# Neighbourhood attention two blocks at a time, in an order of TensorE's queue written out by hand

## The chip, the cores and the metric

The kernel runs on one core of one Trainium2 chip, as one program. The metric is device time in microseconds (us), the median of several runs. TensorE (PE in the profile) multiplies, VectorE (DVE), ScalarE (ACT) and GpSimd (POOL) do the rest, SyncE (SP) issues the DMAs. Each engine runs its own queue in order and waits on semaphores.

## What is computed

Two layers of a hybrid network over 1024 latent tokens (a grid of 16 rows by 64 columns) and 256 context tokens, width 1024, all in f32. Each layer: norm and modulation; one input projection; an mLSTM group and a neighbourhood attention group side by side (8 heads of 64 each); an output projection; a squared-ReLU MLP. The part that matters here is the attention:

```python
def row_block(r):                       # one row of the grid, 64 queries
    rs = jnp.clip(r - kr_n // 2, 0, rows - kr_n)
    ...
    s_loc = jnp.einsum('bhqd,bhrkd->bhqrk', q_r, k_r) + bias      # 8 rows of keys
    s_loc = jnp.where(col_mask[:, None, :], s_loc, -jnp.inf)      # 16 columns of them
    s_ctx = jnp.einsum('bhqd,bhcd->bhqc', q_r, kch)               # 256 context keys
    p = jax.nn.softmax(jnp.concatenate([s_loc, s_ctx], -1), axis=-1)
    return einsum(p_loc, v_r) + einsum(p_ctx, vch)
...
if need_ctx:                            # layer 0 alone: the context attends to itself
    pc = jax.nn.softmax(einsum('bhqd,bhkd->bhqk', qch, kch), axis=-1)
```

## The kernel before

All the tokens' activations lie transposed in SBUF, 128 features to a tile, in three groups of columns: group 0 (context, 256 columns), groups 1 and 2 (latent tokens, 512 each). Every large product is made of three matmuls of rounded parts (lines 86 to 88: high by high, low by high, high by low), so each operand needs a cast on ACT (the high part) and a subtraction on DVE (the low part). One projection of a group (`qk_project`) is 24 matmuls, 256 or 512 wide, into one PSUM bank.

The attention of a layer (`na`) works through four pairs of heads. For each pair, `na_qk` yields up to six steps, one projection each: keys of groups 0, 1, 2, then queries of groups 0, 1, 2 (layer 1 has no queries of group 0, so five steps). After a projection, ACT and DVE cast it out of its bank. For the keys these are L729 and L730; for the queries L742 and L743 on ACT and two subtractions L745 on DVE, first for head 0, then the same again for head 1.

A pair has ten blocks of 128 queries in layer 0 (two of context, then eight tiles of the grid) and eight in layer 1. A block (`na_block`) has three stages, and the generator stops between them:

- scores: PE multiplies queries by context keys (L853, four matmuls) and by local keys (L863, four); DVE takes the negated maximum (L858, L864); ACT exponentiates (L868); DVE scales by the reciprocal sum (L869, L870). The bias comes by DMA into the tile `S` beforehand (L775).
- transposes: ten on PE (L878, L889, L897), four for a block of context; copies out of PSUM to `pc` (ACT), `pl` (DVE, L890) and `pl3` (ACT, L898).
- values: ten matmuls into one bank (L904), 64 columns of TensorE for each head; the trace has two records for each. DVE copies the result to `nyT` (L784).

The loop of `na` first runs all steps of pair 0's `na_qk`. Then, for each block, it moves the block two places back to its transposes, starts the scores of the new block, takes one step of the next pair's `na_qk` and runs the values of the block two places back. In the last pair that step is one of `ahead`, which loads output weights and the finished rows of `y` and makes the first four tiles of the output projection. Code order is only a priority: a scheduler (Tile) plans the order on every engine from its own costs, and may put any instruction earlier or later. So the projections of a pair lie a whole pair ahead of their use, and PE's order is the planner's.

There are eight PSUM banks: six of tag `q`, two of tag `mm` (after the start of a layer, projections use `mm`).

Of the kernel before, what the change touches and what calls it, by code (L numbers as in the profile page):

```python
# [25 lines left out]
KT = D // 128  # L26
# [20 lines left out]
class Kern:  # L47
# [700 lines left out]
    def na_blocks(self, l, pr, need_ctx):  # L748
# [17 lines left out]
        for hf in range(2):  # L766
            R, r0 = NROWS[hf], ROWS0[hf]
            yT = np_.tile([128, 512], F32, name="nyT", bufs=2)
            for cb in range(4):
# [6 lines left out]
                vt = np_.tile([128, 3, 128], F32, name="vt", bufs=3)  # L776
# [39 lines left out]
    def na(self, l, hi, lo, need_ctx, Wq, accs, last):  # L816

        run_all(self.fill)
        run_all(self.rows)
        self.wide = 1  # L820
        run_all(self.na_qk(l, 0, hi, lo, need_ctx, Wq, accs))
        self.wide = 0
        pending = []
        for pr in range(4):
            nxt = self.na_qk(l, pr + 1, hi, lo, need_ctx) if pr < 3 else last
            for n, blk in enumerate(self.na_blocks(l, pr, need_ctx)):
                if len(pending) == 2:
# [12 lines left out]
        for blk in pending:  # L840
            next(nxt, None)
            run_all(blk)
        run_all(nxt)

    def na_block(self, q, krhs, k, Rw, tb, vt, vc, put):
# [36 lines left out]
        if nl:  # L882
# [7 lines left out]
            nc.vector.tensor_copy(pl[:kw].rearrange("p a t -> p (a t)"), tp[:kw, :])  # L890
# [17 lines left out]
    def load_y(self, l, gi, hi, lo, ks=range(KT)):  # L908
# [949 lines left out]
```

## Time and profile before

| | |
|---|---|
| median of 3 runs | 2882.88 us (2878.18 to 2883.33) |
| span of the profiled execution, first to last instruction | 2883.5 us |
| PE busy | 2833.7 us, 98% |
| DVE busy | 2216.7 us, 77% |
| ACT busy | 1262.9 us, 44% |
| mean granted TensorE clock | 0.998 |

The page gives the profiled execution by its span; no time of its own stands beside it. The span lies 0.6 us above the median of the runs. A matmul's record shows its whole passage through the array (273 ns for a short one), and the records overlap, so the work done is read from the distance of starts and not from the busy time. Attention runs from about 457 to 690 us in layer 0 and from 1963 to 2190 us in layer 1.

### The profile page before, as it was taken

What the parts mean: (1) busy time and instruction counts of PE and PEld (TensorE: products, weight loads), DVE (VectorE), ACT (ScalarE), POOL (GpSimd) and SP (SyncE); (2) the same over time, 40 slices, a digit from 0 to 9 for tenths busy, and PEclk for the clock granted to TensorE, in tenths of its full rate; (3) what the DMA queues carried; (4) which work ended last, traced back from release to release, by engine and by line L of the source; (5) the groups of instructions that cost most, each with busy time, mean ns of one, the idle gap of its engine ahead of it and who ended that gap; (6) DMA issues with size and microseconds to landing.
All of it is one profiled execution on the core that took longest, in us unless ns stands there. A gap on an engine that the chain in (4) does not pass through costs nothing. (4 is left out here: it accounts for less than half of the span.)

```text
span 2883.5 us, 45724 instructions
## 1 busy us (share of the span) xinstructions
PE 2833.7 (98%) x16644; PEld 2402.4 (83%) x16644; DVE 2216.7 (77%) x5097; ACT 1262.9 (44%) x2426; POOL 67.3 (2%) x117
## 2 busy tenths in 40 slices
PE   8999999999999999999999999999999999999998
PEld 5888888888888888888889988888878788888888
DVE  7789987885798777599877778877786887759774
ACT  5333334564553333344544333335565533334453
POOL 0000000001000000000000000000010000000000
PEclk9999999999999999999999999999999999999999
DMA  7433332246447555798977222223256454478673
GB/s 248 164 123 105 113 115 78 91 125 217 150 157 235 188 197 198 273 334 288 313 260 252 67 88 73 74 62 105 88 169 199 132 190 144 154 252 312 212 252 102
DMA packets 278946, 497.42 MB, mean 173 GB/s; under 512 B 23328, under 2 KB 119584, under 8 KB 278720
## 3 DMA queue, kind: packets, MB, share of 16 engines
q1 hardware_dynamic: 278720, 494.49, 51.7%
q8 instruction: 131, 2.15, 0.3%
q14 instruction: 95, 0.78, 0.1%
HBM read 398.82 MB, written 95.59 MB: 171 GB/s over the span
## 5 line engine op out<-in xcount | busy, mean ns | idle before, releaser
L86 PE MATMUL q<-ah,whi 128*128 128x512 f32 (+1 forms) x1480 | 551.8, 373 | 2.6 <-ACT ah L955 1.9
L88 PE MATMUL q<-ah,wlo 128*128 128x512 f32 (+1 forms) x1480 | 550.2, 372 | 1.3 <-DVE wlo L956 1.3
L87 PE MATMUL q<-al,whi 128*128 128x512 f32 (+1 forms) x1480 | 550.7, 372 | 0.0
L86 PE MATMUL mm<-ah,whi 128*128 128x512 f32 (+1 forms) x1112 | 382.8, 344 | 1.5 <-ACT ah L914 1.5
L87 PE MATMUL mm<-al,whi 128*128 128x512 f32 (+1 forms) x1112 | 382.4, 344 | 0.4 <-DVE al L915 0.4
L88 PE MATMUL mm<-ah,wlo 128*128 128x512 f32 (+1 forms) x1112 | 382.1, 344 | 0.5 <-DVE wlo L81 0.5
L86 PEld LDWEIGHTS q<-ah,whi 128*128 128x128 f32 x1480 | 278.8, 188 | 52.3 <-ACT ah L955 2.7
L88 PEld LDWEIGHTS q<-ah,wlo 128*128 128x128 f32 x1480 | 278.8, 188 | 51.3 <-DVE wlo L956 2.1
L87 PEld LDWEIGHTS q<-al,whi 128*128 128x128 f32 x1480 | 278.9, 188 | 48.9 <-issue 1.4
L86 PE MATMUL mm<-whi,ah 128*128 128x512 f32 (+2 forms) x864 | 313.3, 364 | 0.9 <-DVE st L312 0.4
L87 PE MATMUL mm<-wlo,ah 128*128 128x512 f32 (+2 forms) x864 | 309.5, 359 | 0.2 <-DVE wlo L81 0.2
L88 PE MATMUL mm<-whi,al 128*128 128x512 f32 (+2 forms) x864 | 308.2, 357 | 0.0
L86 PEld LDWEIGHTS mm<-ah,whi 128*128 128x128 f32 x1112 | 210.5, 189 | 27.9 <-ACT ah L914 1.9
L88 PEld LDWEIGHTS mm<-ah,wlo 128*128 128x128 f32 x1112 | 210.6, 189 | 25.6 <-DVE wlo L81 1.0
L87 PEld LDWEIGHTS mm<-al,whi 128*128 128x128 f32 x1112 | 210.5, 189 | 25.0 <-DVE al L915 0.5
L955 ACT CAST ah<-raw 128x512 fp32r<-128x512 f32 (+1 forms) x264 | 142.9, 566 | 120.7 <-PE q L88 58.3
L86 PEld LDWEIGHTS mm<-whi,ah 128*128 128x128 f32 x864 | 163.6, 190 | 28.0 <-issue 3.1
L88 PEld LDWEIGHTS mm<-whi,al 128*128 128x128 f32 x864 | 163.8, 190 | 23.0 <-issue 0.7
L87 PEld LDWEIGHTS mm<-wlo,ah 128*128 128x128 f32 x864 | 163.9, 190 | 22.3 <-DVE wlo L81 0.4
L956 DVE TENSOR_TENSOR al<-raw,ah 128x512 fp32r<-128x512 f32 (+1 forms) x264 | 157.6, 621 | 23.5 <-ACT ah L955 23.0
L956 DVE TENSOR_TENSOR wlo<-raw,whi 128x1024 fp32r<-128x1024 f32 x84 | 102.4, 1222 | 74.4 <-ACT whi L955 71.9
L86 PE MATMUL q<-th,whi 128*128 128x512 f32 x384 | 150.5, 392 | 2.2 <-DVE s L1120 2.0
(287 smaller groups left out, 5249.4 us busy)
## 6 DMA issues: line engine op xcount, KB each, us to landing
raw<-w SPq DMA_DIRECT2D x168, 512.0 KB
raw<-hid SPq DMA_DIRECT2D x104, 512.0 KB
wada<-w_adaT SPq DMA_DIRECT2D x96, 512.0 KB
wraw<-w SPq DMA_DIRECT2D x80, 512.0 KB
hid<-hb SPq DMA_DIRECT2D x128, 256.0 KB
hid<-ht SPq DMA_DIRECT2D x96, 256.0 KB
gb<-gscr SPq DMA_DIRECT2D x36, 512.0 KB
wada<-w_ada SPq DMA_DIRECT2D x32, 512.0 KB
```

Source lines behind the costliest of these rows:

```text
L86: mm(out, lh, rh, start=start, stop=False, skip_group_check=True)
L87: mm(out, lh, rl, start=False, stop=False, skip_group_check=True)
L88: mm(out, ll, rh, start=False, stop=stop, skip_group_check=True)
L955: ins = self.nc.scalar.copy(hi, src)
L956: self.nc.vector.tensor_sub(lo, src, fview(hi))
```

## The change

1. The code of the blocks moves to `na_pairs`, which takes two blocks as a unit. For each new block, one block of the unit before it is transposed and the new one's scores are made; when both are through, the values of both blocks of the unit before run back to back.
2. Everything in `na_pairs` stands under `manual_schedule(engines={PE})`: PE's queue has exactly the order of the code there. The other engines are still planned.
3. Before the blocks only four steps of pair 0's projections run (layer 0: the keys and the queries of group 0; layer 1: the keys and the queries of group 1). The remaining queries of a pair are projected inside that pair, behind its blocks 0 and 2 (layer 1: behind block 0). The first four steps of the next pair follow behind blocks 4, 5, 7, 9 (layer 1: 2, 4, 5, 7).
4. `ahead` fetches the output weights a step before they are cast and loads `y` into two buffers of its own. Each of its output tiles is one unbroken run on PE.
5. The copy to `pl` moves from DVE to ACT; `vt` has five buffers, not three.

```diff
-                vt = np_.tile([128, 3, 128], F32, name="vt", bufs=3)
+                vt = np_.tile([128, 3, 128], F32, name="vt", bufs=5)
...
     def ahead(self, l, gi, xsrc, yh, yl, W, xt):
-        for i, _ in enumerate(self.w_out(l, 0, W)):
-            self.load_y(l, gi, yh, yl, range(2 * i, min(2 * i + 2, KT - 1)))
+        raw = []
+
+        def fetch():
+            raw.append(self.wp.tile([128, 1024], F32, name="wraw", bufs=WRAW))
+            self.nc.sync.dma_start(raw[-1][:], self.d["w_out"][l, len(raw) - 1])
+
+        for _ in range(WRAW):
+            fetch()
+        yield
+        for i in range(WB):
+            W.append(self.split_raw(raw[i], 1024))
+            if len(raw) < WB:
+                fetch()
+            self.load_y(l, gi, yh, yl, range(2 * i, min(2 * i + 2, KT - 1)), self.np_)
             yield
...
-            if f % 2:
-                yield
-        self.load_y(l, gi, yh, yl, range(KT - 1, KT))
+        self.load_y(l, gi, yh, yl, range(KT - 1, KT), self.np_)
+        yield
...
+        own = [self.na_qk(l, pr, hi, lo, need_ctx, *((Wq, accs) if pr == 0 else ())) for pr in range(4)]
         self.wide = 1
-        run_all(self.na_qk(l, 0, hi, lo, need_ctx, Wq, accs))
+        for _ in range(4):
+            next(own[0])
         self.wide = 0
-        pending = []
+        with self.tc.manual_schedule(engines={mybir.EngineType.PE}):
+            self.na_pairs(l, need_ctx, own, last)
+
+    def na_pairs(self, l, need_ctx, own, last):
+        behind, pair = [], []
+        mine, others = ((0, 2), (4, 5, 7, 9)) if need_ctx else ((0,), (2, 4, 5, 7))
         for pr in range(4):
-            nxt = self.na_qk(l, pr + 1, hi, lo, need_ctx) if pr < 3 else last
             for n, blk in enumerate(self.na_blocks(l, pr, need_ctx)):
-                if len(pending) == 2:
-                    next(pending[0])
+                if behind:
+                    next(behind[n % 2])
                 next(blk)
-                pending.append(blk)
-                if pr < 3 or not need_ctx or n > 1:
-                    next(nxt, None)
-                if len(pending) > 2:
-                    run_all(pending.pop(0))
-            if pr < 3 or not need_ctx:
-                run_all(nxt)
-        for blk in pending:
+                pair.append(blk)
+                if n in mine:
+                    next(own[pr])
+                elif pr < 3 and n in others:
+                    next(own[pr + 1])
+                if pr == 3 and n:
+                    next(last, None)
+                if len(pair) == 2:
+                    for b in behind:
+                        run_all(b)
+                    behind, pair = pair, []
+            run_all(own[pr])
+        for blk in behind:
             next(blk)
...
-            nc.vector.tensor_copy(pl[:kw].rearrange("p a t -> p (a t)"), tp[:kw, :])
+            nc.scalar.copy(pl[:kw].rearrange("p a t -> p (a t)"), tp[:kw, :])
...
-            y = self.wp.tile([128, 1024], F32, name="wraw", bufs=WRAW)
+            y = pool.tile([128, 512], F32, name="yraw", bufs=2) if pool else self.wp.tile(...)
```

On PE, the order outside the two attention stages is the same before and after. The three places below show the order within. In the names, `ah`, `al` are the activations' high and low parts, `whi`, `wlo` the weights', `nqc` and `nq` the cast queries of group 0 and of groups 1 and 2, `nk` the cast keys, `consts` the identity of a transpose. In the rows of the changed kernel L876 and L886 are the scores (L853 and L863 before), L901, L912 and L920 the transposes (L878, L889, L897), L927 the values (L904).

First place: PE at the start of layer 0's attention, before. The last matmuls of the query projection of group 0 are followed by both other query projections.

```order
L86 MATMUL q<-ah_108,whi 128x256
L87 MATMUL q<-al_132,whi 128x256
L88 MATMUL q<-ah_108,wlo 128x256
L86 MATMUL q<-ah_88,whi 128x512
...
L88 MATMUL mm<-ah_110,wlo 128x512
L853 MATMUL q<-nk_5110,nqc 128x256 x2
L853 MATMUL q<-nk_5111,nqc 128x256 x2
L86 MATMUL mm<-ah_87,whi 128x256
```

The same place after: the scores of block 0 (on `nqc`) stand right behind the projection that makes `nqc`, and those of block 2 (the first on `nq`) two short stages behind the projection that makes that `nq`.

```order
L88 MATMUL q<-ah_108,wlo 128x256
L876 MATMUL q<-nk_5110,nqc 128x256 x2
L876 MATMUL q<-nk_5111,nqc 128x256 x2
L86 MATMUL mm<-ah_88,whi 128x512
...
L88 MATMUL mm<-ah_109,wlo 128x512
L876 MATMUL q<-nk_5110,nqc 128x256 x2
L876 MATMUL q<-nk_5111,nqc 128x256 x2
L901 MATMUL q<-consts,S 128x128 x4
L876 MATMUL q<-nk_5110,nq 128x256 x2
L876 MATMUL q<-nk_5111,nq 128x256 x2
```

What moved: two runs of 24 matmuls, 512 wide, from ahead of the first scores to behind them. Layer 1 starts in the same way, with `nq` of group 1.

Second place: PE between pairs 0 and 1 of layer 1, after. The projection of pair 1's queries of group 1 is the run of 512-wide matmuls at the top; `nk_21024` and `nk_21025` are pair 1's keys, so the last rows are the scores of its block 0.

```order
L88 MATMUL mm<-ah_15377,wlo 128x512
L927 MATMUL q<-pc,vc 64x128 x4
...
L927 MATMUL q<-pl_21397,vt 64x128 x2
L901 MATMUL q<-consts,S 128x128 x4
L912 MATMUL q<-consts,S 128x128 x4
L920 MATMUL q<-consts,S 128x128 x2
L876 MATMUL q<-nk_21024,nq 128x256 x2
```

Before, that projection stood behind an earlier block of pair 0, with the values, transposes and scores of several blocks between it and its use. Now the values of two blocks and the transposes of one lie between.

Third place: PE in the middle of pair 0 of layer 0, before.

```order
L904 MATMUL q<-pc,vc 64x128 x4
L904 MATMUL q<-pl,vt 64x128 x4
L904 MATMUL q<-pl_5632,vt 64x128 x2
L878 MATMUL q<-consts,S 128x128 x4
L889 MATMUL q<-consts,S 128x128 x4
L897 MATMUL q<-consts,S 96x128 x2
```

The same place after: the values of two blocks without a break, then the transposes.

```order
L927 MATMUL q<-pc,vc 64x128 x4
L927 MATMUL q<-pl,vt 64x128 x4
L927 MATMUL q<-pl_5589,vt 64x128 x2
L927 MATMUL q<-pc,vc 64x128 x4
L927 MATMUL q<-pl,vt 64x128 x4
L927 MATMUL q<-pl_5641,vt 64x128 x2
L901 MATMUL q<-consts,S 128x128 x4
L912 MATMUL q<-consts,S 96x128 x4
```

What moved: the values of every second block, up to those of its partner. Counted over both layers, PE's order enters a run of values 75 times before (42 in layer 0, 33 in layer 1) and 37 times after (20 and 17).

More of the change, by code (lines that the diff above doesn't have):

```diff
@@ L819, in na @@
         run_all(self.rows)
+        own = [self.na_qk(l, pr, hi, lo, need_ctx, *((Wq, accs) if pr == 0 else ())) for pr in range(4)]
         self.wide = 1
-        run_all(self.na_qk(l, 0, hi, lo, need_ctx, Wq, accs))
+        for _ in range(4):
+            next(own[0])
         self.wide = 0
-        pending = []
+        with self.tc.manual_schedule(engines={mybir.EngineType.PE}):
[3 more added lines that the diff above has]
+        mine, others = ((0, 2), (4, 5, 7, 9)) if need_ctx else ((0,), (2, 4, 5, 7))
         for pr in range(4):
-            nxt = self.na_qk(l, pr + 1, hi, lo, need_ctx) if pr < 3 else last
             for n, blk in enumerate(self.na_blocks(l, pr, need_ctx)):
-                if len(pending) == 2:
-                    next(pending[0])
+                if behind:
+                    next(behind[n % 2])
                 next(blk)
-                pending.append(blk)
-                if pr < 3 or not need_ctx or n > 1:
-                    next(nxt, None)
-                if len(pending) > 2:
-                    run_all(pending.pop(0))
-            if pr < 3 or not need_ctx:
-                run_all(nxt)
-        for blk in pending:
+                pair.append(blk)
[11 more added lines that the diff above has]
+        for blk in behind:
             next(blk)
-        for blk in pending:
-            next(nxt, None)
+        for blk in behind:
+            next(last, None)
             run_all(blk)
-        run_all(nxt)
+        run_all(last)
     def na_block(self, q, krhs, k, Rw, tb, vt, vc, put):
@@ L905, in na_block, with load_y @@
         put(yp)
-    def load_y(self, l, gi, hi, lo, ks=range(KT)):
+    def load_y(self, l, gi, hi, lo, ks=range(KT), pool=None):
         nc = self.nc
@@ L911, in load_y @@
         for k in ks:
[L912 removed]
+            y = pool.tile([128, 512], F32, name="yraw", bufs=2) if pool else self.wp.tile([128, 1024], F32, name="wraw", bufs=WRAW)
             nc.sync.dma_start(y[:, :n], self.yscr[l][k * 128:(k + 1) * 128, g0:g0 + n])
```

## The prediction

> **What bounds the kernel now.** I read the page's first part, then busy time by stretch over the two attention stages, then PE, DVE and ACT in order of time where the changed order differs. The page's busy line shows one engine nearly always at work:
>
> ```profile
> PE 2833.7 (98%) x16644; PEld 2402.4 (83%) x16644; DVE 2216.7 (77%) x5097; ACT 1262.9 (44%) x2426; POOL 67.3 (2%) x117
> ```
>
> So only PE time counts: matmuls, switches between kinds of matmul, waits. The rows by stretch of layer 0's and layer 1's attention (columns: stretch, length, busy PE, PEld, DVE, ACT, POOL, clock, DMA):
>
> ```profile
> 457.00:690.00 233.00, 227.05 (x1878) 196.39 (x1877) 181.20 (x591) 137.17 (x319) 14.22 (x14) 1.00 0.36 107
> 1963.00:2190.00 227.00, 222.20 (x1715) 188.72 (x1714) 173.93 (x520) 128.62 (x271) 9.21 (x7) 1.00 0.40 124
> ```
>
> PE idles 233.00 - 227.05 = 5.95 and 227.00 - 222.20 = 4.80 us there, 10.75 together. Idle time understates a loss, since a record lasts longer than its turn. One wait in PE's timeline of layer 0, and the same products without one:
>
> ```profile
> 619.88 0.43 PE L863 MATMUL q<-nk,nq 128*128 128x288 f32 x2
> 620.89 0.53 PE L863 MATMUL q<-nk,nq 128*128 128x288 f32 x2 [0.58 <-ACT pc L879]
> ...
> 631.96 0.71 PE L853 MATMUL q<-nk,nq 128*128 128x256 f32 x4
> 632.51 0.69 PE L863 MATMUL q<-nk,nq 128*128 128x288 f32 x4
> 633.04 0.28 PE L86 MATMUL mm<-ah,whi 128*128 128x256 f32 x1
> ```
>
> Two products held PE from 619.88 to 620.89, 1.01 us; four take 632.51 to 633.04, 0.53, so two 0.27. The loss is 0.74 us for 0.58 shown, a factor 1.28. (Scores over the context take 631.96 to 632.51, 0.55 for four.) All waits are then 10.75 x 1.28 = 13.7 us. They lie where no projection fills PE: late in a pair and in the last pair.
>
> **Fewer visits to the value products.** PE's timeline around a lone block's values, and around two blocks' values in a row, which the planner made once, at the end of layer 1:
>
> ```profile
> 616.46 0.39 PE L87 MATMUL mm<-al,whi 128*128 128x512 f32 x1
> 616.69 0.39 PE L88 MATMUL mm<-ah,wlo 128*128 128x512 f32 x1
> 617.01 0.66 PE L904 MATMUL q<-pc,vc 128*64 128x128 f32 x8
> 617.50 0.83 PE L904 MATMUL q<-pl,vt 128*64 128x128 f32 x12
> 618.25 0.66 PE L878 MATMUL q<-consts,S 128*128 128x128 f32 x4
> 618.75 0.60 PE L889 MATMUL q<-consts,S 128*128 128x128 f32 x4
> ...
> 2176.35 0.60 PE L878 MATMUL q<-consts,S 128*128 128x128 f32 x4
> 2176.79 0.60 PE L889 MATMUL q<-consts,S 128*128 128x128 f32 x4
> ...
> 2178.63 0.66 PE L904 MATMUL q<-pc,vc 128*64 128x128 f32 x8
> 2179.11 0.83 PE L904 MATMUL q<-pl,vt 128*64 128x128 f32 x12
> 2179.77 0.61 PE L904 MATMUL q<-pc,vc 128*64 128x128 f32 x8
> ```
>
> Entering costs 0.09 us (616.69 to 617.01 is 0.32, the matmul before took 0.23). Leaving costs 0.09 (twelve records take 0.75 before a transpose, 0.66 before more values) and the four transposes behind take 0.50 instead of 0.44. That is 0.24 us a visit. The order has 75 visits before and 37 after: 38 x 0.24 = **-9.1 us**, all on PE. Bounds: 0.18 without the transposes (-6.8) and 0.30 with a slow first pair (-11.4, an estimate).
>
> **Waits that go.** The changed order spreads the projections: a 24-matmul run stands in nearly every unit of two blocks, and the output tiles of the last pair are fed by loads issued earlier. I take all 13.7 us as gone, **-13.7**, and set new waits against it. The bounds are -13.7 and, if half return, -6.9.
>
> **Waits that come: queries cast too late.** Here the change puts a projection just ahead of its user. The price is the time from a projection's last matmul to its last subtraction. ACT's, DVE's and PE's rows at layer 0's start, then ACT's, DVE's and PE's at layer 1's:
>
> ```profile
> 449.58 0.37 ACT L742 CAST nqc<-q 64x256 fp32r<-64x256 f32 x1 [1.66 <-DVE nqc L745]
> 451.40 0.58 ACT L742 CAST nq<-q 64x512 fp32r<-64x512 f32 x1 [1.07 <-PE q L88]
> 454.03 0.58 ACT L742 CAST nq<-q 64x512 fp32r<-64x512 f32 x1 [1.45 <-DVE nq L745]
> ...
> 447.95 0.69 DVE L730 SCALAR_TENSOR_TENSOR nk<-q,nk 64x512 fp32r<-64x512 f32 x1 [0.31 <-ACT nk L729]
> 448.68 0.87 DVE L745 TENSOR_TENSOR nqc<-q,nqc 64x256 fp32r<-64x256 f32 x2
> 450.36 0.89 DVE L745 TENSOR_TENSOR nqc<-q,nqc 64x256 fp32r<-64x256 f32 x2 [0.81 <-ACT nqc L743]
> 452.61 1.38 DVE L745 TENSOR_TENSOR nq<-q,nq 64x512 fp32r<-64x512 f32 x2 [1.37 <-ACT nq L743]
> 455.25 1.40 DVE L745 TENSOR_TENSOR nq<-q,nq 64x512 fp32r<-64x512 f32 x2 [1.26 <-ACT nq L743]
> ...
> 445.73 0.40 PE L86 MATMUL q<-ah,whi 128*128 128x512 f32 x1
> 451.20 0.39 PE L86 MATMUL mm<-ah,whi 128*128 128x512 f32 x1
> ```
>
> ```profile
> 1958.32 0.58 ACT L742 CAST nq<-q 64x512 fp32r<-64x512 f32 x1 [1.33 <-PE q L88]
> 1962.19 1.42 DVE L745 TENSOR_TENSOR nq<-q,nq 64x512 fp32r<-64x512 f32 x2 [1.26 <-ACT nq L743]
> 1958.12 0.39 PE L86 MATMUL q<-ah,whi 128*128 128x512 f32 x1
> ```
>
> ACT's casts for head 1 wait until DVE has subtracted for head 0, so the chain is serial: 451.40 to 456.65 and 1958.32 to 1963.61, 5.3 us, plus 0.2 us behind the last matmul. PE filled it with the next projection (445.73 to 451.20 is one, 5.47 us).
>
> - *Layer 0, block 0.* ACT's and DVE's order is unchanged up to here, so the trace gives the time itself: the projection ends at 445.73, head 0's `nqc` is ready at 449.55, head 1's at 451.25. With 0.27 for its products the scores end at 451.5 instead of 446.3 (445.73 + 0.55): **+5.2 us**, with nothing to fill it.
> - *Layer 0, block 2.* The next projection then ends near 457.0. Only block 1's scores (0.55) and four transposes (0.44) lie between. The chain, with block 1's maximum on DVE ahead of it, ends near 462.7 (an estimate: 457.0 + 0.2 + 5.3 and 0.2 of delay); the scores end near 463.5, and 459.1 was due: **+4.4**.
> - *Layer 1, block 0.* Ready at 1963.61 after a projection that ends at 1958.12; the scores end near 1964.4 where 1959.2 was due: **+5.2**.
> - *Layer 1, block 0 of pairs 1 to 3.* Cover: values of two blocks (1.24 + 1.14), ten transposes (0.50 and six at 0.11, 1.16), head 0's context scores (0.27), 3.8 us; chain 5.5: **3 x 1.7 = +5.1**.
> - *Layer 0, block 2 of pairs 1 to 3.* Cover: ten transposes, context scores, values of two blocks, four transposes, with head 0's scores of block 2 (0.27) 4.8 us; chain 5.5 and 0.1 of delay: **3 x 0.8 = +2.4**.
>
> If ACT and DVE ran the two heads side by side, the chain would be 0.2 + 4 x 0.58 and one subtraction (0.7) with some delay, 3.4 us: the low bound of all five. The high bound is another 0.5 us each for DVE's other work.
>
> **Free edits.** The copy to `pl` takes DVE 0.69 us and ACT takes 0.58 us for the same shape:
>
> ```profile
> L890 DVE COPY pl<-q 128x512 f32<-128x512 f32 x16 | 11.0, 689 | 3.2 <-PE q L889 3.1
> L879 ACT COPY pc<-q 128x512 f32<-128x512 f32 x40 | 23.1, 578 | 11.7 <-PE q L878 11.1
> ```
>
> ACT has the room: it is busy 137 of 233 us. In a unit with no projection it has little: three units (one in layer 0's last pair, two in layer 1's) may wait about 1 us each, as the pair of rows at 619.88 does: **+3**, between 0 and 6. The weight and `y` loads move on SP's queue past the bias loads; their users come several stages later, so 0. `vt`'s buffers: 0.
>
> **The granted clock.** Busy time by stretch around two short PE droughts elsewhere in this trace, with the wait in the second:
>
> ```profile
> 1624.80:1628.20 3.40, 1.48 (x9) 1.04 (x10) 3.32 (x9) 1.19 (x4) 0.10 (x1) 1.00 0.87 271
> 1628.20:1631.60 3.40, 3.40 (x18) 3.40 (x18) 2.87 (x3) 2.10 (x3) 0.00 (x0) 0.52 0.09 37
> 2276.80:2280.20 3.40, 2.45 (x8) 1.02 (x6) 3.40 (x7) 3.40 (x7) 0.00 (x0) 1.00 0.53 154
> 2283.60:2287.00 3.40, 1.37 (x7) 0.83 (x6) 3.40 (x7) 0.00 (x0) 0.00 (x0) 1.00 0.01 2
> 2287.00:2290.40 3.40, 3.40 (x9) 2.63 (x10) 3.40 (x7) 1.79 (x3) 0.00 (x0) 0.52 0.00 0
> 2286.84 0.59 PE L86 MATMUL q<-th,whi 128*128 128x512 f32 x1 [2.03 <-DVE s L1120]
> ```
>
> After 3.4 us in which PE was busy 1.4 to 1.5, the clock was 0.52 for the next 3.4; after 2.45 busy it stayed at 1.00. Half speed for 3.4 us loses 1.6 us. The three long waits (5.2, 4.4, 5.2) each make such a stretch: **3 x 1.6 = +4.8**, between 0 and 8.
>
> The Trainium skill, page "TensorE: Matmul & The Clock Gate", section "HAM oscillation — how this bites in real kernels", gives the rule as: no idle gap of PE over about 3.4 us. The trace differs, since a longest gap of 2.03 us was enough. By the page only layer 0's block 0, with one unbroken gap of 3.7 us, would pay, and the sum would be 3.2 us lower.
>
> **The sum.** -9.1 - 13.7 + 5.2 + 4.4 + 5.2 + 5.1 + 2.4 + 3.0 + 4.8 = +7.3 us on the span of 2883.5, 2890.8; the span is 0.6 above the runs' median, so 2890. A measurement of this kernel can tell about 0.2%, 5.8 us, from no change.
>
> **Rivals.**
> - *Faster.* The casts of the two heads run side by side in the new plan. The chain is 3.4 us, 2.1 less: the five terms become 3.1, 2.3, 3.1, 0 and 0, the clock drops once, 1.6: -22.8 + 8.5 + 3.0 + 1.6 = -9.7, 2873. It decides below a chain of about 3.8 us. Against it: both chains quoted were serial. Chance 0.12.
> - *No change: the clock holds.* The waits come, but each holds a few matmuls in its middle (head 0's scores), and only the unbroken gap halves the clock: 2890 - 3.2, 2887. This is what the page's rule makes of it. For it: head 0 is ready halfway. Against: the 2.03 us gap. With milder waits at the pairs' borders, the cases within 0.2% have 0.33.
> - *Slower still.* The fixed order makes many small waits, since PE can no longer put a projection's matmuls into a hole; half of the 13.7 us stay: 2897. For it: before, the planner split output tiles around such holes. Chance 0.15; the forecast itself has 0.40.
>
> The range 2878 to 2902 runs from the sum without the clock, the 3.0 and the 2.4 and with -11.4 for the visits (-5.2, 2878) to half of the old waits, twice the new 3.0 and one more halving of the clock (+18.8, 2902).
>
> **What would show it.** Right: PE idle for over 4 us between layer 0's first query projection and the second, and again ahead of block 2's scores; over 4 us ahead of layer 1's first scores; releasers DVE `nq` and `nqc`; the clock below 1 behind them; 37 visits; little idle late in the pairs. Wrong: short chains (DVE `nq` soon after the projection), a clock of 1.00 throughout, or old waits on `pc`, `pl` and `S` in full.

## The result, and the profile after

The changed kernel takes 2924.22 us (median of 4 runs, 2921.61 to 2927.05) against 2882.51 us before: a ratio of 1.0146, 95% interval 1.0132 to 1.0161. It is 41.7 us slower, and 2890 us was forecast, with 2902 as the upper end. The profiled execution took 2923.64 us, its span 2921.9.

The page's busy line after, and the rows by stretch that answer to those of before (columns as there):

```profile
PE 2842.3 (97%) x16644; PEld 2415.5 (83%) x16644; DVE 2180.9 (75%) x5033; ACT 1292.3 (44%) x2490; POOL 67.4 (2%) x117
```

```profile
457.00:690.00 233.00, 214.50 (x1715) 187.39 (x1715) 157.30 (x526) 144.22 (x327) 14.54 (x14) 0.99 0.34 102
1963.00:2190.00 227.00, 212.73 (x1593) 183.93 (x1593) 153.04 (x499) 135.82 (x293) 9.03 (x7) 0.97 0.39 117
```

PE idles 18.5 us in the first stretch, where it idled 5.95, and 14.3 in the second, where it idled 4.80; its clock is below 1 in both. (Both stages now end behind these stretches: PE's last value products start at 708.5 and 2209.6 us.) PE does the same matmuls, so three that stand in the same order on both sides give the loss by stage. They are the last products ahead of each layer's query projections and one behind layer 1's attention, first in PE's timeline of before, then of after:

```profile
442.64 0.38 PE L678 MATMUL q<-consts,hs 128*128 128x128 f32 x2
1952.43 0.39 PE L678 MATMUL q<-consts,hs 128*128 128x128 f32 x2
2220.15 1.02 PE L268 MATMUL mm<-ssq,ones 128*128 128x512 f32 x2
```

```profile
442.79 0.38 PE L678 MATMUL q<-consts,hs 128*128 128x128 f32 x2
1973.32 0.39 PE L678 MATMUL q<-consts,hs 128*128 128x128 f32 x2
2259.59 1.02 PE L268 MATMUL mm<-ssq,ones 128*128 128x512 f32 x2
```

Ahead of layer 0's attention the two are 0.15 us apart, behind its layer 20.9, behind layer 1's attention 39.4. The loss lies in the two attention stages and just behind them.

**The starts: as forecast, and a longer half clock.** PE's timeline after, at layer 0's start:

```profile
445.75 0.28 PE L88 MATMUL q<-ah,wlo 128*128 128x256 f32 x1
449.38 1.00 PE L876 MATMUL q<-nk,nqc 128*128 128x256 f32 x2 [3.35 <-DVE nqc L745]
450.98 1.10 PE L876 MATMUL q<-nk,nqc 128*128 128x256 f32 x2 [0.60 <-DVE nqc L745]
451.88 0.63 PE L86 MATMUL mm<-ah,whi 128*128 128x512 f32 x1
456.57 0.43 PE L88 MATMUL mm<-ah,wlo 128*128 128x512 f32 x1
...
461.81 0.38 PE L876 MATMUL q<-nk,nq 128*128 128x256 f32 x1 [1.15 <-DVE nq L745]
464.55 0.58 PE L876 MATMUL q<-nk,nq 128*128 128x256 f32 x1 [1.58 <-DVE nq L745]
466.59 0.63 PE L86 MATMUL mm<-ah,whi 128*128 128x512 f32 x1
```

Block 0's scores end at 451.88; without a wait they would end at 446.4 (445.75, one matmul, 0.55), so 5.5 us late. The matmuls behind them follow each other at 0.43 us and not 0.23 (452.31 is the second) up to 456.6: 2.3 us lost to the clock. Block 2's scores are late by 5.1 us, and 1.7 us of half clock follow. Layer 1 starts in the same way, 5.9 us late, with this row as its longest wait and 1.6 us of half clock behind it; the second row is ACT's at layer 0's start, where head 1's casts still wait for head 0's subtractions:

```profile
1981.14 0.39 PE L876 MATMUL q<-nk,nq 128*128 128x256 f32 x1 [1.98 <-DVE nq L745]
...
449.71 0.37 ACT L742 CAST nqc<-q 64x256 fp32r<-64x256 f32 x1 [1.66 <-DVE nqc L745]
```

Rows by stretch show the granted clock at these three places, and at a fourth that comes below. It is 0.50 for 6.8 us each time:

```profile
449.80:456.60 6.80, 6.18 (x15) 4.61 (x16) 2.60 (x10) 1.74 (x6) 0.00 (x0) 0.50 0.34 96
463.45:470.25 6.80, 5.47 (x15) 4.43 (x16) 4.30 (x14) 1.85 (x5) 0.00 (x0) 0.50 0.00 0
1982.40:1989.20 6.80, 5.17 (x14) 4.19 (x15) 4.30 (x14) 2.13 (x6) 0.00 (x0) 0.50 0.47 139
2149.65:2156.45 6.80, 6.04 (x16) 4.85 (x17) 4.08 (x14) 3.17 (x8) 1.28 (x1) 0.50 0.65 197
```

The first part of each falls on the late scores themselves and is counted with them; the 2.3, 1.7 and 1.6 us are only what the projection behind them loses.

**The bare stretches: what I had not seen.** Between the projection behind block 2 and the one behind block 4, PE has only transposes, scores and values in layer 0. PE's timeline there in pair 1, then ACT's:

```profile
540.02 0.66 PE L927 MATMUL q<-pc,vc 128*64 128x128 f32 x8 [0.43 <-ACT pc L902]
541.99 0.64 PE L912 MATMUL q<-consts,S 128*96 128x128 f32 x4 [0.73 <-ACT pc L902]
545.38 0.59 PE L886 MATMUL q<-nk,nq 128*128 128x352 f32 x2 [1.72 <-ACT pl L913]
...
542.56 0.58 ACT L743 CAST nq<-mm 64x512 fp32r<-64x512 f32 x1
543.04 0.80 ACT L891 ACTIVATE S<-S,smax 128x608 f32<-128x608 f32 x1
544.75 0.58 ACT L913 COPY pl<-q 96x512 f32<-96x512 f32 x1
```

All three waits end with copies out of PSUM. The copy at 544.75 could start when its transposes were through at 542.5, but on ACT it stands behind the casts of the queries just projected and two exponentials. ACT had begun these casts late, behind the cast of a weight (537.23, 1.05 us). By the distance of starts PE loses 3.8 us here, and 3.9, 3.8 and 4.4 in the other three pairs. The stretch as a whole, the 54 us behind it, and within these a stretch that has no projection either:

```profile
537.20:545.90 8.70, 5.82 (x48) 4.57 (x47) 6.94 (x18) 6.88 (x13) 0.00 (x0) 1.00 0.44 133
546.00:600.00 54.00, 53.57 (x439) 47.79 (x438) 35.64 (x125) 31.46 (x74) 0.00 (x0) 1.00 0.29 87
568.50:575.50 7.00, 7.00 (x78) 6.64 (x78) 5.34 (x16) 4.95 (x10) 0.00 (x0) 1.00 0.31 99
```

In the first DVE and ACT are each busy for some 80% of the time, feeding each other in turn, and PE for 67%; in the second PE idles for 0.43 us in 54. The third row shows that the missing projection is not the whole matter: behind block 7's projection, of keys, PE works through 78 matmuls and never waits, while ACT is busy for 4.95 us in 7.00. Behind block 2's it has 48, since the values of the two context blocks are short, and ACT and DVE have the casts of the queries as well. Every unit of two blocks has a projection in pairs 0 to 2 of layer 0; the stretch that waits runs across the border of two units.

**The borders of layer 1's pairs.** PE's waits at the first border and in the unit behind it, then the two longest of those at the third, and ACT's row ahead of the casts there:

```profile
2037.87 0.38 PE L876 MATMUL q<-nk,nq 128*128 128x256 f32 x1 [0.81 <-DVE nq L745]
2038.69 0.36 PE L876 MATMUL q<-nk,nq 128*128 128x256 f32 x1 [0.44 <-DVE nq L745]
2047.58 0.59 PE L886 MATMUL q<-nk,nq 128*128 128x352 f32 x2 [0.68 <-ACT pc L902]
...
2147.52 0.38 PE L876 MATMUL q<-nk,nq 128*128 128x256 f32 x1 [0.59 <-DVE nq L745]
2150.17 0.58 PE L876 MATMUL q<-nk,nq 128*128 128x256 f32 x1 [1.49 <-DVE nq L745]
...
2145.06 0.62 ACT L937 CAST ah<-yraw 128x512 fp32r<-128x512 f32 x1 [3.29 <-DMA yraw<-yscr]
```

At the first two borders the scores are 1.8 us late (1.7 was forecast) and the unit behind loses another 1.3. At the third, ACT's queue holds a cast of `y` from `ahead` that waits until 2145.06 for its load, so the casts of the queries start at 2145.59, 2.3 us behind the product that follows their projection (0.1 us at the first border): the scores are 4.5 us late, 2.0 us of half clock follow, and the unit behind again loses 1.3.

**Behind layer 1's attention.** PE's wait, the casts on ACT that it and the loads wait for, and SP's weight loads:

```profile
2240.94 0.50 PE L86 MATMUL mm<-ah,whi 128*128 128x512 f32 x1 [3.64 <-ACT whi L80]
...
2208.44 1.05 ACT L80 CAST whi<-wraw 128x1024 fp32r<-128x1024 f32 x1 [5.86 <-PE mm L87]
2239.84 1.04 ACT L80 CAST whi<-wraw 128x1024 fp32r<-128x1024 f32 x1 [2.98 <-DMA wraw<-w_out]
...
2193.72 10.48 SPq L73 DMA_DIRECT2D wraw<-w_out  x2
2234.46 0.33 SPq L73 DMA_DIRECT2D wraw<-w_out  x1
```

The second half of the output weights is cast when the first output tiles give their buffers back (the row at 2208.44 was released by a matmul). Two of these tiles now stand behind the last values, so the two loads at 2193.72 hold SP for 10.48 us, all later loads come late, and PE waits 3.64 us for a weight that was issued at 2234.46. With the half clock behind it this costs 5.3 us.

### The profile page after: what moved, and what is told of

It reads as the page before. It is cut to its first block, busy times and chain, and to the rows that moved or that the text cites. A ratio compares the mean times of both kernels' runs of the same rounds, so it can differ in the third digit from the quotient of the medians.

```text
span 2921.9 us, 45716 instructions
## 1 busy us (share of the span) xinstructions
PE 2842.3 (97%) x16644; PEld 2415.5 (83%) x16644; DVE 2180.9 (75%) x5033; ACT 1292.3 (44%) x2490; POOL 67.4 (2%) x117
## 5 line engine op out<-in xcount | busy, mean ns | idle before, releaser
L86 PE MATMUL q<-ah,whi 128*128 128x512 f32 (+1 forms) x1464 | 545.6, 373 | 1.5 <-ACT ah L978 1.4
L88 PE MATMUL q<-ah,wlo 128*128 128x512 f32 (+1 forms) x1464 | 543.9, 372 | 1.0 <-DVE wlo L979 0.9
L87 PE MATMUL q<-al,whi 128*128 128x512 f32 (+1 forms) x1464 | 544.5, 372 | 0.0
L86 PE MATMUL mm<-ah,whi 128*128 128x512 f32 (+1 forms) x1128 | 392.2, 348 | 3.6 <-ACT whi L80 3.6
L88 PE MATMUL mm<-ah,wlo 128*128 128x512 f32 (+1 forms) x1128 | 391.2, 347 | 0.5 <-DVE wlo L81 0.5
L87 PE MATMUL mm<-al,whi 128*128 128x512 f32 (+1 forms) x1128 | 391.1, 347 | 0.0
L81 DVE TENSOR_TENSOR wlo<-wraw,whi 128x1024 fp32r<-128x1024 f32 (+2 forms) x90 | 107.7, 1199 | 76.3 <-ACT whi L80 62.0
```

The lines of the kernel that those rows point to most:

```text
L81: nc.vector.tensor_sub(lo[:, :n], raw[:, :n], fview(hi[:, :n]))
L86: mm(out, lh, rh, start=start, stop=False, skip_group_check=True)
L87: mm(out, lh, rl, start=False, stop=False, skip_group_check=True)
L88: mm(out, ll, rh, start=False, stop=stop, skip_group_check=True)
```

## The experiments

Each kernel is the changed one with the edit shown, unless it says otherwise. Times are medians; before took 2881.9 to 2882.6 us beside them.

**1. A projection inside the bare stretch.**

```diff
-        mine, others = ((0, 2), (4, 5, 7, 9)) if need_ctx else ...
+        mine, others = ((0, 2), (3, 5, 7, 9)) if need_ctx else ...
```

> One number changed: in layer 0 the next pair's first projection (keys of group 0, 24 matmuls 256 wide, 2.86 us of PE) stands behind block 3 and not behind block 4. Theory A (the loss is where PE has nothing but scores, transposes and values between two projections while ACT and DVE still work through a cast chain; in layer 0 that is from block 2's projection to block 4's, 3.8 to 4.4 us in each of four pairs): a projection inside this stretch covers 2 to 2.9 us of it in pairs 0 to 2 (pair 3 has none), so 6 to 9 us less than the changed kernel, 2915 to 2918 us. Theory B (ACT is the late engine, since it also copies pl): the same ACT work has to be done in the same place, the waits move on by two blocks, 2922 to 2926 us.

2916.82 us, ratio 1.0127 (1.0110 to 1.0143): 7.4 us less than the changed kernel. PE's timeline in the same stretch of pair 1 shows the waits that are left:

```profile
545.07 0.44 PE L901 MATMUL q<-consts,S 128*128 128x128 f32 x2 [0.61 <-DVE S L893]
546.24 0.42 PE L920 MATMUL q<-consts,S 128*96 128x128 f32 x2 [0.29 <-ACT pc L902]
```

By starts the stretch loses 2.0 us instead of 3.8. So a missing cover (independent work that PE can do while it would wait) made about half of the loss there, with ACT's amount of work unchanged: theory A. The other half are waits that stay with the projection in place.

**2. The copy to `pl` back on DVE.**

```diff
-            nc.scalar.copy(pl[:kw]..., tp[:kw, :])
+            nc.vector.tensor_copy(pl[:kw]..., tp[:kw, :])
```

> The changed kernel with the copy to pl back on DVE, nothing else. Theory B (ACT's queue is late by this copy): the waits that end with the copy to pl go, 2.1 us in each of four pairs of layer 0 and 1.8 us at each of three borders in layer 1, about 14 us, 2908 to 2912 us. Theory A (projections are missing as cover, whichever engine copies): DVE is as busy there with subtractions and maxima, the waits stay within 4 us, 2920 to 2928 us.

2932.69 us, ratio 1.0178 (1.0163 to 1.0193): 8.5 us more. Both theories missed: B has the wrong sign, and A expected next to nothing. PE's waits in the last pair's bare stretch of layer 0:

```profile
669.00 0.66 PE L927 MATMUL q<-pc,vc 128*64 128x128 f32 x8 [0.43 <-ACT pc L902]
674.27 0.59 PE L886 MATMUL q<-nk,nq 128*128 128x352 f32 x2 [1.64 <-DVE nyT L761]
```

The long wait is as long, but DVE now ends it. The loss lies elsewhere: PE's order is the same in both kernels, and matmul by matmul the two profiled executions part by 5.6 us in layer 0's attention, 3.8 of them in the last pair, and by another 5.4 in layer 1's. So part 5 of the change, which I had priced at 0, is a gain of 8.5 us inside this order.

**3. No fixed order on PE.**

```diff
-        with self.tc.manual_schedule(engines={mybir.EngineType.PE}):
-            self.na_pairs(l, need_ctx, own, last)
+        self.na_pairs(l, need_ctx, own, last)
```

> The changed kernel without the fixed order on PE: the code is the same, but the planner may split projections and put their matmuls into holes, as it does before block 0 and around the context's values of layer 0. There are then 56 visits to the value products and not 37. Theory A: the planner fills the stretches that have no projection, so most of the 16 us of layer 0's four stretches and of the 18 us at the starts goes, and 19 visits at 0.24 us (4.6 us) come back: 2888 to 2900 us. Theory B (ACT too late): the holes can't be filled for free, 2910 to 2925 us.

2889.67 us, ratio 1.0030 (1.0018 to 1.0042): 34.6 us less, with 56 visits to the values instead of 37. The same two rows by stretch:

```profile
457.00:690.00 233.00, 229.79 (x1897) 202.12 (x1897) 162.72 (x549) 150.89 (x345) 14.84 (x14) 1.00 0.38 114
1963.00:2190.00 227.00, 222.02 (x1690) 189.75 (x1690) 150.96 (x469) 139.07 (x296) 9.00 (x7) 0.99 0.41 126
```

PE idles 3.2 and 5.0 us, where it idled 5.95 and 4.80 before the change. The planner puts single matmuls of a projection between the first scores and between the products of the bare stretches. What is left of the loss lies behind layer 1's attention, where PE waits for a weight as in the changed kernel:

```profile
2205.30 0.79 PE L86 MATMUL mm<-ah,whi 128*128 128x512 f32 x1 [3.70 <-ACT whi L80]
```

Ahead of this wait the profiled execution is 1.5 us ahead of the kernel before, behind it and its half clock 4.6 us late.

**4. Queries projected a pair ahead, order still fixed.**

```diff
-        for _ in range(4):
+        for _ in range(5):
             next(own[0])
...
-        mine, others = ((0, 2), (4, 5, 7, 9)) if need_ctx else ((0,), (2, 4, 5, 7))
+        mine, others = ((1,), (3, 4, 6, 7, 9)) if need_ctx else ((0,), (2, 3, 4, 6))
...
-                if n in mine:
+                if pr == 0 and not need_ctx and n in (0, 2):
+                    if n == 0:
+                        next(own[1])
+                elif n in mine:
                     next(own[pr])
```

> The changed kernel, fixed order and two blocks at a time, with other places for the projections: queries of group 1 one pair ahead (layer 0: steps behind blocks 3, 4, 6, 7 and 9 of the pair before, and only the last queries behind block 1 of their own; layer 1: behind 2, 3, 4, 6, and the last queries behind block 0; all five steps of layer 1's pair 0 ahead of its blocks). So no product uses a query whose projection stands right ahead of it, and in pairs 0 to 2 each unit of two blocks has a projection. Theory A: the waits at both starts (5.6, 5.2 and 5.9 us), those at the borders (12 and 6 us), the clock's share (7.6 us) and three of layer 0's four bare stretches (12 us) go, up to 54 us, less new waits of 5 to 10 in the last pairs: 2872 to 2885 us. Theory B: under half of it goes, since ACT has the same work, 2900 to 2915 us.

2896.68 us, ratio 1.0050 (1.0035 to 1.0065): 27.5 us less, between the two theories. Places alone bring back two thirds of the loss, but not down to before: new waits come in layer 1's first units and in both last pairs, which have lost their projections, and some 6 us behind layer 1's attention are still lost.

**5. The loads of `ahead` as before.**

```diff
-        raw = []
-        ...
+        yield
+        for i, _ in enumerate(self.w_out(l, 0, W)):
+            self.load_y(l, gi, yh, yl, range(2 * i, min(2 * i + 2, KT - 1)))
+            yield
...
-        self.load_y(l, gi, yh, yl, range(KT - 1, KT), self.np_)
+        self.load_y(l, gi, yh, yl, range(KT - 1, KT))
```

> The changed kernel with the loads of ahead as they were before (weights loaded at the step that casts them, y through the two wraw buffers), one empty step ahead so that each step stands behind the same block as in the changed kernel. Theory A (part 4 moved the loads of the second half of the output weights and of group 2's rows of y to after the attention of layer 1; PE waits 3.64 us there and its clock halves behind it): the 5.3 us that the changed kernel loses between 2193 and 2250 us, and most of the 1.4 us at 815 us, go: 2916 to 2920 us. Theory D (the loads come late because the attention ends late, whatever the code of ahead): no change, 2922 to 2927 us.

2925.82 us, ratio 1.0147 (1.0131 to 1.0164): no change, and the 5.3 us behind layer 1's attention are still there. The loads themselves are not the cause. (The 0 is a balance: in the profiled execution the wait at layer 1's last border is 1.4 us shorter, and one in layer 0's last block 3.5 us longer.)

**6. Both: no fixed order and the old loads** (edits 3 and 5).

> The last one's edit together with the planner's order on PE (no fixed order). The run without the fixed order alone took 2889.7 us and lost 6 to 8 us behind layer 1's attention. Theory A: these go, 2881 to 2885 us. Theory D: 2887 to 2892 us.

2894.19 us, ratio 1.0036 (1.0023 to 1.0049). Again no gain from the old loads. It confirms 5.

**7. The values block by block, order still fixed.**

```diff
                 if behind:
+                    if n % 2:
+                        run_all(behind[0])
                     next(behind[n % 2])
```

> The changed kernel in its fixed order, but the values of each unit's first block run right before the transposes of the second, not together with its values: 73 visits to the values instead of 37, all else in place. The prediction's price of 0.24 us a visit gives 36 x 0.24 = 8.6 us more, 2931 to 2935 us. The rival: a visit costs nothing that waits don't hide, or a result that is ready earlier frees its bank earlier and shortens waits by as much: 2918 to 2926 us.

2931.44 us, ratio 1.0178 (1.0157 to 1.0199): 7.2 us more. Its trace has 71 visits, 34 more, so 0.21 us each, where the prediction's price was 0.24, bounded by 0.18 and 0.30. The pairing does save PE time: the slowest run with it took 2927.05 us, the fastest without it 2931.09. But 0.21 is a net, with the intervals of two kernels in it, and the waits moved too: at layer 1's first border the scores lose 3.2 us, not 1.8, and the bare stretches of pairs 1 and 2 lose less.

**8. Before, with the copy to `pl` on ACT alone** (edit of part 5 in the kernel before).

> The kernel before with one edit: the copy to pl runs on ACT, not DVE (part 5 alone). In the changed kernel the reverse edit cost 8.5 us. Theory A (DVE is the later of the two engines in all waits): 2 to 8 us less than before, 2875 to 2881 us, since before has only 13.7 us of waits. Theory B: ACT gets late instead, 2883 to 2890 us.

2883.97 us, ratio 1.0006 (0.9996 to 1.0015): the same. Where projections cover the chain, it does not matter which engine copies, so the 8.5 us of run 2 belong to the changed order.

**9. All of pair 0's queries ahead of the blocks.**

```diff
-        for _ in range(4):
-            next(own[0])
+        for _ in own[0]:
+            pass
...
-                    next(own[pr])
+                    next(own[pr], None)
```

> The changed kernel with all projections of pair 0's queries ahead of the blocks of each layer, as before the change; pairs 1 to 3 and everything else as changed. Theory A: the waits at the starts (5.6 and 5.2 us in layer 0, 5.9 in layer 1) and the half clock behind them (2.3, 1.7 and 1.6 us) go, 22 us; pair 0 then lacks two projections as cover in layer 0 and one in layer 1, and gives 4 to 10 us back: 2906 to 2913 us. The rival (waits only move, since ACT and DVE bound these stretches): 2916 to 2925 us.

2908.15 us, ratio 1.0087 (1.0073 to 1.0101): 16.1 us less. The starts and the clock behind them are confirmed as causes. In layer 0 some 6 us came back as new waits, the longest in PE's timeline where block 0's first transposes wait for its own softmax and no projection is left to stand between:

```profile
462.95 1.08 PE L901 MATMUL q<-consts,S 128*128 128x128 f32 x4 [3.31 <-DVE S L893]
```

Pair 0's bare stretch has no projection now either, but no casts of queries fall into it: its wait of 1.7 us for the copy to `pl` is gone (pairs 1 to 3 keep theirs), and the longest wait there is 0.69 us.

**10. Before, with only the pairing and the copy on ACT.** `vt` has five buffers; the queries, `ahead` and the planner are those of before.

```diff
-                if len(pending) == 2:
-                    next(pending[0])
+                if len(pending) == 2:
+                    done.append(pending.pop(0))
+                    next(done[-1])
...
-                if len(pending) > 2:
-                    run_all(pending.pop(0))
+                if len(done) == 2:
+                    for b in done:
+                        run_all(b)
+                    done = []
```

> The kernel before with two parts of the change alone: the values of two blocks back to back (a block is transposed two places behind its scores as before, and the values wait until two blocks are through), and the copy to pl on ACT, with vt in five buffers. Queries stay a pair ahead, PE is planned, ahead is as before. 52 visits, not 75. Theory A (the late projections and the bare stretches made the loss, the pairing itself is a gain): 23 visits at 0.20 to 0.24 us less, 4.6 to 5.5 us, 2875 to 2880 us, if the old waits stay. Theory E (taking two blocks at a time makes waits of its own, since bunched values leave PE longer without a result ready): 2885 to 2895 us.

2882.46 us, ratio 0.9999 (0.9990 to 1.0008): the same as before, though it makes 52 visits and not 75. In its profiled execution PE is some 4 us ahead of before at the end of layer 1's attention and 0.6 at its last stage. In between, a wait for a weight's cast takes 1.54 us instead of 0.74, with the clock at 0.50 behind it (2303.7 to 2307.0 us), where before has 1.00, and a wait for a cast of activations 1.45 instead of 0.24. Whether the gain is given back there in every run is not settled by one profile; this execution was the slowest of eleven.

**11. The same, with the next pair's steps behind every second block** (`n % 2 == 0`).

> The last kernel, with the steps of the next pair behind every second block (0, 2, 4, 6, 8, the rest at the pair's end) and not behind the first five or six: each unit of two blocks has a projection. 47 visits. Theory A: 28 visits at 0.20 to 0.24 us, 5.6 to 6.7 us, and half of the old waits outside the last pairs, 3 to 6 us, less than before: 2870 to 2875 us. Theory E: 2882 to 2895 us.

2891.43 us, ratio 1.0025 (1.0015 to 1.0036). Theory A missed by 16 us. An even spread gives each unit one projection, and yet PE waits 3.25 us ahead of one set of transposes in layer 0's last pair (643.23 us) and 3.10 us ahead of one in layer 1's (2134.48 us). Why these waits come is not shown.

**12. Layer 1's output tiles ahead of the last values.**

```diff
+        if not need_ctx:
+            run_all(last)
         for blk in behind:
             next(blk)
```

> The changed kernel, but in layer 1 all the output tiles of ahead stand ahead of the last two blocks' transposes and values (as in the kernel before), not between and behind them. Theory F (the second half of the output weights is cast when the output tiles give their buffers back, and the rows of y of group 2 are loaded behind those weights through the same two buffers; with two tiles behind the last values all of this is late): the 5.3 us lost between 2193 and 2250 us go, and 1 to 2 us of waits at the last values, which lose their cover, come: 2919 to 2922 us. Rival D (it is late because the attention ends late): 2923 to 2928 us.

2918.07 us, ratio 1.0122 (1.0106 to 1.0137): 6.2 us less. The row of the end of layer 1's attention and the time behind it, and SP's loads:

```profile
2186.00:2240.00 54.00, 54.00 (x306) 44.65 (x305) 26.25 (x46) 22.96 (x41) 0.00 (x0) 1.00 0.54 171
```

```profile
2193.65 8.34 SPq L73 DMA_DIRECT2D wraw<-w_out  x2
2230.12 0.33 SPq L73 DMA_DIRECT2D wraw<-w_out  x1
```

PE is never idle there now, at full clock; the weight that was issued 41 us behind the first pair of loads goes out 36 us behind it. The two loads hold SP for 8.34 us here too, so that hold by itself is not the cause; what moved is the tiles. Theory F holds.

**13 and 14. A better table, fixed and planned.**

```diff
-        mine, others = ((0, 2), (4, 5, 7, 9)) if need_ctx else ((0,), (2, 4, 5, 7))
         for pr in range(4):
+            if need_ctx:
+                mine, others = 3 if pr == 3 else 1, (3, 4, 6, 7, 9)
+            else:
+                mine, others = (9, 2, 2, 2)[pr], (0, 2, 4, 6) if pr == 0 else (0, 4, 5, 6)
+            load = (0, 1, 2, 3, 4, 6, 7, 8, 9) if need_ctx else (0, 1, 3, 4, 6, 7)
...
```

Five steps of pair 0's projections run ahead of the blocks, and layer 1's output tiles stand ahead of the last values. Kernel 14 leaves `manual_schedule` out.

> A fixed order with other places: queries one pair ahead as in the run with early queries, but layer 1's pair 0 has a projection in every unit; the last queries of the last pair come later (behind block 3 in layer 0, 2 in layer 1), so that the bare stretches of the last pairs are split; the loads of ahead start a pair earlier and its tiles run ahead of the last values. The run with early queries took 2896.7 us. Theory A with F: 5 us behind layer 1's attention, 3 to 4 at its start, 4 to 6 in the last pairs go: 2881 to 2886 us, the same as before. If the stiff order as such costs (theory S): 2888 to 2897 us.

> The same code as the last, planned on PE, 48 visits. Theory S: at least 5 us under the fixed order, since the planner fills the holes that are left. Theory A (the places are all that matters): within 4 us of the fixed order, 2878 to 2888 us.

Fixed: 2893.52 us, ratio 1.0038 (1.0025 to 1.0050). Planned: 2883.77 us, ratio 1.0003 (0.9994 to 1.0012). The rows by stretch, first fixed, then planned:

```profile
457.00:690.00 233.00, 225.69 (x1892) 200.04 (x1891) 166.06 (x564) 154.11 (x354) 14.71 (x14) 1.00 0.37 111
1963.00:2190.00 227.00, 218.03 (x1696) 190.15 (x1695) 151.29 (x483) 138.61 (x295) 9.26 (x7) 0.98 0.38 117
```

```profile
457.00:690.00 233.00, 230.42 (x1910) 203.51 (x1909) 166.44 (x564) 154.59 (x355) 14.72 (x14) 1.00 0.39 116
1963.00:2190.00 227.00, 222.75 (x1706) 193.09 (x1705) 152.55 (x485) 141.05 (x302) 9.02 (x7) 0.98 0.39 120
```

The same code is 9.8 us faster when the planner may break a projection open, though it visits the values 48 times and not 36: PE idles 6.8 us in the two stretches and not 16.3 (in an execution of 2889.64 us, above the planned kernel's median). A stiff order costs something of its own (theory S). No kernel tried beats before.

**15 and 16. Edits 1, 9 and 12 together, and then the border.** In 16 layer 1's table is `(2, 4, 5, 6)`, not `(2, 4, 5, 7)`.

> The changed kernel with the three edits that each brought time back, together: all of pair 0's queries ahead of the blocks (alone 16.1 us less), layer 0's next keys behind block 3 (alone 7.4 less), layer 1's output tiles ahead of the last values (alone 6.2 less). If these are separate places: 2924.2 - 29.7 = 2894.5, within 3 us. If they share waits: 2899 to 2908 us.

> The last kernel, and in layer 1 the projection of the next pair's queries of group 1 stands behind block 6, not 7: the next pair's first scores follow after a block and two blocks' values, no longer after the values and one block's transposes. In the changed kernel the borders' waits are 3.0, 3.0 and 6.0 us of PE and 2.0 us of half clock behind the third. Theory A: 6 to 10 us less than the last kernel. The rival (the wait moves to the stretch without a projection behind block 7): within 3 us of it.

15: 2900.15 us, ratio 1.0061 (1.0046 to 1.0076), 24.1 us less than the changed kernel where the three alone sum to 29.7: the places share waits. 16: 2897.98 us, ratio 1.0053 (1.0036 to 1.0070), within 3 us, as the rival said. PE's longest wait at the last border, in 15, and the longest in the units behind it, in 16:

```profile
2132.42 0.38 PE L878 MATMUL q<-nk,nq 128*128 128x256 f32 x1 [1.49 <-DVE nq L745]
```

```profile
2140.08 0.60 PE L888 MATMUL q<-nk,nq 128*128 128x352 f32 x2 [2.25 <-ACT pc L904]
```

The long wait for queries is gone, and waits that end with a copy out of a bank come in the units that have lost their projection.

## Why the prediction was wrong

The sign and four of the mechanisms were right; the size was not. Term by term, in us, with the measured price by distances of starts in the profile, or from the run named:

| term | forecast | measured |
|---|---|---|
| fewer visits | -9.1 | -8.0 (0.21 a visit in run 7, a net, times 38) |
| old waits go | -13.7 | not separable; 0.43 idle in 54 us behind the first bare stretch |
| layer 0, block 0 | +5.2 | +5.5 |
| layer 0, block 2 | +4.4 | +5.1 |
| layer 1, block 0 | +5.2 | +5.9 |
| layer 1's borders | +5.1 | +12 (3, 3 and 6) |
| layer 0, later pairs' starts | +2.4 | +5.9 (some 2.4 of it at block 2, as forecast) |
| units without a projection | +3.0 | +16 in layer 0, +3.6 in layer 1 |
| clock | +4.8 | +7.6, in four places |
| moved loads, behind layer 1 | 0 | +5.3 |

With the forecast's -13.7 the measured column sums to about +45; the two spans differ by 38.4. What the 7 us between them are is not shown: the undisturbed distances that were taken off are estimates. The column tells sizes, not a balance.

- **The step that failed most** is the paragraph "Free edits", "In a unit with no projection it has little: three units ... may wait about 1 us each ... +3, between 0 and 6". I counted units in the last pairs and overlooked that the changed table leaves a stretch without a projection in every pair of layer 0, though it stands in PE's order. The sentence under "Waits that go", that a projection "stands in nearly every unit", was true but does not reach this, since the stretch runs from one unit into the next. And I priced it by one copy's wait, where a weight's cast, the casts of a 512-wide projection, exponentials and copies of three blocks all pass through ACT and DVE while PE has 4.6 us of work (the same products and transposes by their undisturbed distances, an estimate). Four times 4 us is nearly half of the error. Run 1 puts work for PE into the stretch, run 9 takes the casts of the queries out of it, and either shortens the wait.
- **The chains of casts** were sized well: 5.2, 4.4, 5.2 against 5.5, 5.1, 5.9, and run 9 removes them. The rival "casts of the two heads run side by side" is out: ACT's cast at 449.71 waited for DVE's subtraction, as before the change.
- **The borders**: the wait itself was 1.8 us where 1.7 was forecast. Left out were the unit behind it, which loses 1.3 us, most of it to a copy that comes late, and the last border, where a cast of `y` waits for its load in ACT's queue and holds the casts of the queries for 2.2 us.
- **The clock**: halved behind all three long waits, as forecast, and behind a fourth, the last border. How long was wrong: 6.8 us each time, where I had reckoned with 3.4, the length before (rows from 1628.20 and from 2287.00). That the term still came out near 1.6 us a place is luck: the first part of each half clock fell on PE's waiting and on the late scores. Only layer 0's block 0 has one unbroken gap (3.35 us). The rival by the Trainium skill, page "TensorE: Matmul & The Clock Gate", section "HAM oscillation — how this bites in real kernels" (an idle gap of over some 3.4 us), would have had one halving at most; with gaps of at most 1.98 us at layer 1's start and 1.58 at block 2 the trace shows one each. The trace disagrees with the page there.
- **The moved loads** cost 0 on balance, as I said (runs 5 and 6). The 5.3 us come from the output tiles that the written order puts between and behind the last values (run 12). The prediction speaks of users "several stages later" and looked at loads alone, not at the buffers that a tile gives back.
- **Part 5** was priced at 0 and is worth 8.5 us in the changed order (run 2), 0 in the old one (run 8).
- **"Slower still"** named the right cause, PE can no longer put a projection's matmuls into a hole, but gave it half of the old waits as its price. Run 3 measures all of it at 34.6 us, of which run 4 gets 27.5 by other places, and runs 13 and 14 put 9.8 us on the stiffness alone.

What stays open: why run 10, with 23 visits less and no late projection, gains nothing that can be measured; and no run takes run 3's planner and run 12's places together in the changed kernel, so whether they would come down to before is not shown.

## What to carry to other kernels

When an order is fixed by hand, go through the bound engine's order for every stretch between two pieces of long independent work, and set against it the time of the other engines' whole chain there: casts, exponentials and copies out of PSUM together, not the one wait that is in sight. A hole without long independent work is not a loss by itself: it waits where the other engines' chain in it is longer than the bound engine's own work. Cover is a fixed stock: moving a projection into one hole opened another in runs 9 and 16, and the planner, which may split a projection, filled several in runs 3 and 14, though not in run 11. A saving on the bound engine (about 0.2 us a visit) counts only if the order that buys it does not use up that cover.

## What the runs showed of the hardware

- The granted clock fell to half without a long gap: behind waits of at most 1.98 us in layer 1 and 1.58 us in layer 0, with a few matmuls between them. Behind the 3.35 us gap, and at three more places, it stayed at half for 6.8 us (449.8 to 456.6 at the first), where the rows of the prediction show 0.52 for 3.4 us before the change.
- One more visit to the value products costs 0.21 us when read from the time of the whole kernel (7.2 us for 34, other waits having moved too), a little under the 0.24 that the starts in the trace gave.
